# Groups by seven products in a macaron channel mixer: two products accumulate onto banks whose contents were copied, and two splits change place

## The chip, the core and the metric

The kernel runs on one core of one Trainium2 chip. The metric is device time in microseconds of that core, the median of several executions. TensorE (PE) multiplies, VectorE (DVE) and ScalarE (ACT) work elementwise and read what TensorE leaves in PSUM, GpSimd (POOL) and SyncE (SP) mostly issue transfers. PSUM has eight banks of 128 x 512 float32 values here.

## The reference

Two layers over 256 tokens of width 1024. Each layer is a SwiGLU channel mixer at half weight, an attention part, and a second SwiGLU mixer; so there are four passes of the mixer. The change is in the mixer alone:

```
def swiglu(h, w_gate, w_up, w_down):
    return (jax.nn.silu(h @ w_gate) * (h @ w_up)) @ w_down
...
x = x + 0.5 * swiglu(rms_norm(x, ffn1_norm[l]), ffn1_w_gate[l], ffn1_w_up[l], ffn1_w_down[l])
```

`h` is 256 x 1024, the gate and up weights 1024 x 2816, the down weights 2816 x 1024, all float32.

## The kernel before

**Precision.** Every weight and activation is split into a high part (a cast to the fast float format on ScalarE) and a low part (the rest, a subtraction on VectorE). A product is three matmuls for each block of 128: high by high, low by high, high by low. A "split" below is half of a loaded weight block: one cast of 128 x 1024 values on ScalarE and one subtraction of that size on VectorE.

**Groups.** The 2816 hidden columns are taken in five groups of 512 (g = 0 to 4) and a narrow one of 256. Each group makes its hidden block h, and the down projection of a group runs inside the next one. Four PSUM banks hold the output of the down projection for the whole pass; four banks are left for everything else.

**Groups by seven products.** A group's gate and up projections for two blocks of 128 tokens are a two by two block product. In the groups listed in `SEVEN` (2 to 4 in the first pass, 1 to 4 in the other three, 15 in all) it is done with seven products in place of eight, from sums of weights and sums of activations. The weight sums are made by transfers that add on their way (issued by POOL, `gather`) and by additions on VectorE (`plus`); the activation sums by `make_sums`, whose fourth tile is named `v`, so that the seventh product is the only one with `ps<-w,v` in a trace. `prod` makes one product: 12 matmuls into a fresh bank. `by_seven` (line 634) runs for g > 1: first product, copy to m1; seventh product, copy to m7; the transposes of the former h (`turn`, which also splits the down operands: two casts, two low parts); second product, and g0 = second + m1; third product; the first half of the down projection (24 matmuls); fifth and sixth product; u2 = sixth - m1, u3 = m7 + u2; fourth product, g1 = fourth - u3; the last three subtractions and additions with the fifth and third product; the two `up` multiplications that make h; the second half of the down projection. For g = 1 the order differs: first product, half the transposes, second product, the other half, down projection, third product, seventh product with its copy, then fifth, sixth, fourth. g0 passes through SiLU on ScalarE: in the first pass behind the third product, in the other passes behind the first half of the down projection (`run` is true there).

**Order.** In the mixer each engine runs its instructions in the order in which the program text issues them. `weights()` takes the next weight block and calls `ahead(n)`, which issues splits up to number n, the additions that prepare them, and loads into free ones of six raw buffers. Block i has the splits 2i and 2i + 1. A plain `weights()` goes to 2i + look, and the product itself goes one further in its middle (`Split.part`); `held=True` leaves the latter out, and the first argument of `weights` lowers the former. `look` is 8 less one for each group by seven behind the first in passes two to four (8 for g = 1, 5 for g = 4), and 6, then 5, in the first pass. Loads go out on SyncE's queue when a raw buffer is free, and the adding transfers on POOL's.

**Buffers.** m1, m7, g0 and the other 128 x 512 temporaries share five buffers (`tmp`).

Of the kernel before, what the change touches and what calls it, by code (L numbers as in the profile page):

```python
# [12 lines left out]
ALU = mybir.AluOpType  # L13
# [21 lines left out]
def trunk(ctx: ExitStack, tc: tile.TileContext, x, n1, g1, u1, d1, nm, w_in, sink,  # L35
# [21 lines left out]
    pe, act, dve, pool = Kept(nc.tensor), Kept(nc.scalar), Kept(nc.vector), Kept(nc.gpsimd)  # L57
# [9 lines left out]
    def nm_(s):  # L67
        uid[0] += 1
        return f"{s}_{uid[0]}"

    def bank():
        return ps.tile([P, 512], F32, tag="ps", bufs=8, name=nm_("ps"))
# [4 lines left out]
    def blk(dt=F32R):  # L77
        return s4.tile([P, 2, 512], dt, tag="s4", name=nm_("s4"))

    def tmp(tag="tmp", bufs=5, shape=(P, 2, 256), dt=F32):  # L80
        return tp.tile(list(shape), dt, tag=tag, bufs=bufs, name=nm_(tag))
# [143 lines left out]
    look = [IN_MIX]  # L225
    at = dict(use=0, dma=2, prep=2, split=4)
# [22 lines left out]
    def weights(less=0, held=False):  # L249

        i = at["use"]
        at["use"] += 1
        if i > 1:
            ahead(2 * i + look[0] - less)
        w = loaded[i]
        w.held = held
        return w
# [181 lines left out]
    norm = Norm(0)  # L439
# [162 lines left out]
    def ffn(norm, aside=None, before=None, final=False, sevens=SEVEN[1]):  # L602
        def silu(out_, acc, t):
            act.activation(out_, acc, AF.Silu, scale=norm.r[:, t:t + 1])
            return out_

        def gate(gs):
            g = []
            for t in range(2):
                n = gs[t].shape[1]  # L610
                g.append(silu(tmp().rearrange("p a n -> p (a n)")[:, :n], gs[t], t))
            return g

        def up(h, acc, g, t):
            n = acc.shape[1]
            dve.scalar_tensor_tensor(h[:, t, :n], in0=acc, scalar=norm.hr[:, t:t + 1], in1=g, op0=ALU.mult, op1=ALU.mult)

        def hidden(g, us):
            h = blk(F32)
            for t in range(2):  # L620
                up(h, us[t], g[t], t)
            return h

        def prod(xo, w):
            acc = bank()
            for k in range(4):
                hi, lo = w.part(k)
                xh, xl = xo(k)
                pe.matmul(acc, lhsT=xh, rhs=hi, start=k == 0, stop=False)
                pe.matmul(acc, lhsT=xl, rhs=hi, start=False, stop=False)  # L630
                pe.matmul(acc, lhsT=xh, rhs=lo, start=False, stop=k == 3)
            return acc

        def by_seven(h, g):


            flat = lambda: tmp().rearrange("p a n -> p (a n)")

            def put(o, x, y, op):
                dve.tensor_tensor(o, x, y, op=op)  # L640
                return o

            late, run = g == max(sevens), 1 in sevens
            m1, m7 = flat(), flat()
            if g > 1:
                act.copy(m1, prod(norm.quarter(0, 0), weights()))
                act.copy(m7, prod(norm.summed(3), weights(held=True)))
                hT = turn(h, 2)
                p2 = prod(norm.quarter(0, 1), weights())
                g0 = put(flat(), p2, m1, ALU.add)  # L650
                p3 = prod(norm.summed(2), weights())
                if not run:
                    silu(g0, g0, 0)
                down(hT, g - 1, 0, weights())
                if run:
                    silu(g0, g0, 0)
            else:
                p1 = prod(norm.quarter(0, 0), weights(1, True))
                hT = turn(h, (0,))
                w = weights(1, True)  # L660
                act.copy(m1, p1)
                p2 = prod(norm.quarter(0, 1), w)
                hT += turn(h, (1,))
                g0 = put(flat(), p2, m1, ALU.add)
                down(hT, 0, 0, weights())
                silu(g0, g0, 0)
                p3 = prod(norm.summed(2), weights())
                act.copy(m7, prod(norm.summed(3), weights()))
            h = blk(F32)
            p5 = prod(norm.summed(0), weights())  # L670
            p6 = prod(norm.summed(1), weights(look[0] - 5 if late else run, late or run))
            u2 = put(flat(), p6, m1, ALU.subtract)
            u3 = put(m7, m7, u2, ALU.add)
            p4 = prod(norm.quarter(1, 1), weights(look[0] - 4 if late else 3 * run, late or run))
            g1 = put(m1, p4, u3, ALU.subtract)
            w = weights(look[0] - 3 if late else 2 * run)
            silu(g1, g1, 1)
            put(u3, u3, p5, ALU.subtract)
            put(u2, u2, p5, ALU.subtract)
            put(u2, u2, p3, ALU.add)  # L680
            up(h, u2, g0, 0)
            up(h, u3, g1, 1)
            down(hT, g - 1, 1, w)
            return h

        def turn(hs, n):
            out_ = []
            for i in (range(n) if isinstance(n, int) else n):
                sl = halves(bank())
                for c in range(2):  # L690
                    for t in range(2):
                        pe.transpose(sl[:, c, t * P:(t + 1) * P], hs[:, t, (2 * i + c) * P:(2 * i + c + 1) * P], ident)
                hb = blk()
                split(hb, sl)
                out_.append(hb)
            return out_

        accs = [[bank(), bank()] for _ in range(2)]

        def down(hT, g, h, w):  # L700
            tokens(accs[h], [None] * (2 * g) + hT, w, 4 * g, last=(FC - 1, G4 - 1) if final and h else FC - 1)


        gs, us = [bank(), bank()], [bank(), bank()]
        if before is None:
            before = norm.late
        look[0] = IN_FFN
        before(0)
        ws = (weights(), weights(2))
        for k in (0, 2):  # L710
            if k:
                before(1)
                look[0] = IN_FFN + (1 in sevens)
            for sl, w in zip((gs, us), ws):
                tokens(sl, norm.xs, w, 0, (k, k + 1))
                if k and 1 in sevens:
                    norm.copies(2)
        before(2)
        if 1 in sevens:
            sums = norm.make_sums()  # L720
            next(sums)
            norm.halve()
            w = weights()
            next(sums)
            next(sums)
            tokens(gs, norm.xs, w, 4)
            w = weights(0, True)
            g = gate(gs)
            next(sums)
        else:  # L730
            norm.halve()
            tokens(gs, norm.xs, weights(), 4)
            g = gate(gs)
            w = weights()
        tokens(us, norm.xs, w, 4)
        h = hidden(g, us)
        if 1 in sevens:
            next(sums)
        for n in range(1, NGRP):
            if n in sevens:  # L740
                look[0] = IN_FFN + min(sevens) - n if before is not take_x else IN_MIX - (n == NGRP - 1)
                h = by_seven(h, n)
                continue
            sums = norm.make_sums()
            gs = [bank(), bank()]
            tokens(gs, norm.xs, weights(), 0)
            hT = turn(h, 2)
            norm.copies()
            next(sums, None)
            tokens(gs, norm.xs, weights(), 4)  # L750
            g = gate(gs)
            next(sums, None)
            us = [bank(), bank()]
            for k0 in (0, 4):
                tokens(us, norm.xs, weights(), k0)
                next(sums, None)
            h = hidden(g, us)
            for hh in range(2):
                down(hT, n - 1, hh, weights())
                if hh == 0:  # L760
                    next(sums, None)

        gu = [bank(), bank()]
        tokens(gu, norm.xs, weights(), 0)
        hT = turn(h, 2)
        tokens(gu, norm.xs, weights(), 4)
        h = hidden(gate([b[:, 0:256] for b in gu]), [b[:, 256:512] for b in gu])

        def rest():
            hE = turn(h, 1)  # L770
            if aside is not None:
                aside()
            return hE
        return accs, hT, rest
# [294 lines left out]
    for l in range(DEPTH):  # L1069
# [7 lines left out]
        if not final:  # L1077
            norm = Norm((l + 1) * 8)
# [39 lines left out]
    for c in (0, 256):  # L1118
        acc = bank()[:, 0:256]
# [35 lines left out]
```

## Time and profile before

| what | value |
|---|---|
| median of 3 executions | 925.17 us (923.89 to 926.65) |
| profiled execution | 924.94 us |
| its span, first to last instruction | 923.2 us |
| granted TensorE clock | 0.999 of full speed |
| DMA, mean over the span | 218 GB/s |

A row of the timeline gives start, length, engine, line, operation, output and inputs by the program's names (`w` split weights, `raw` loaded weights, `s` activations and hidden blocks, `q` and `v` activation sums, `tmp` temporaries, `ps` PSUM), shapes and a count; in brackets stands the engine's idle time before it and what ended it. Rows of one kind in a run are merged: the length is then that of the run. Since a helper records all instructions, all have line L50; they are told apart by their tiles. Matmuls overlap, so the length of one (0.39 us) is not the step from one to the next.

### The profile page before, as it was taken

How to read it: one execution, taken by the hardware profiler on the slowest of the kernel's cores; microseconds unless marked ns; L12 is line 12 of the kernel's file. 1: busy time of each engine (PE TensorE's matmuls, PEld its weight loads, DVE VectorE, ACT ScalarE, POOL GpSimd, SP SyncE). 2: the span in 40 equal slices, each digit the busy share in tenths (PEclk: the TensorE clock that was granted, in tenths of full speed). 3: DMA queues.
4: the chain of work that ended last, by engine and by line, in shares of the span. 5: the costliest groups of instructions: out<-in, count | busy, mean ns of one | idle time of the engine just before them, and what ended most of it. 6: DMA issues, size and time to landing. Idle time of an engine off the chain costs nothing.

```text
span 923.2 us, 12580 instructions
## 1 busy us (share of the span) xinstructions
PE 908.6 (98%) x4696; PEld 763.7 (83%) x4696; DVE 807.6 (87%) x1123; ACT 590.6 (64%) x917; POOL 67.7 (7%) x83
## 2 busy tenths in 40 slices
PE   8999999999999999999999999999999999999997
PEld 6888888899888888877888888788998888888786
DVE  6769999969875999999879999997698689999995
ACT  7846575557755776575486676565577496676561
POOL 0501000000000100100010010000001010000011
PEclk9999999999999999999999999999999999999999
DMA  9997897837436698897767998787462467998831
GB/s 334 355 235 208 248 273 266 237 101 221 135 123 182 151 287 245 247 269 263 258 168 200 295 264 235 233 288 227 118 232 92 137 155 202 282 279 243 232 135 47
DMA packets 114061, 200.87 MB, mean 218 GB/s; under 512 B 3662, under 2 KB 31376, under 8 KB 114000
## 3 DMA queue, kind: packets, MB, share of 16 engines
q1 hardware_dynamic: 96528, 166.74, 53.6%
q0 software_dynamic: 16096, 31.75, 19.1%
q10 hardware_dynamic: 1376, 1.57, 0.5%
q8 instruction: 37, 0.61, 0.3%
q14 instruction: 24, 0.20, 0.1%
HBM read 199.00 MB, written 1.05 MB: 217 GB/s over the span
## 4 chain that ended last, share of the span: by engine, by line
PE 85%; DVE 11%; issue 2%; DMA 1%; ACT 1%; SPq 0%; POOLq 0%; POOL 0%; DVEq 0%; ACTq 0%
PE ps L50 85%; DVE w L50 7%; DVE raw L50 2%; DVE tmp L50 1%; DVE s L50 1%; DMA raw<-in_ffn_w_gate_dram 1%; ACT w L50 1%; ACT tmp L50 0%; SPq L156 0%; DVE xk L50 0%; POOLq L1150 0%; POOL rf L50 0%; SPq L422 0%; DVEq L50 0%; ACTq L50 0%
## 5 line engine op out<-in xcount | busy, mean ns | idle before, releaser
L50 PE MATMUL ps<-w,s 128*128 128x512 f32 (+1 forms) x2574 | 602.8, 391 | 1.2 <-ACT w L50 0.5
L50 PEld LDWEIGHTS ps<-w,s 128*128 128x128 f32 x2574 | 477.0, 188 | 102.5 <-DVE w L50 4.3
L50 DVE TENSOR_TENSOR w<-raw,w 128x1024 fp32r<-128x1024 f32 (+1 forms) x458 | 482.7, 1102 | 33.7 <-ACT w L50 32.8
L50 ACT CAST w<-raw 128x1024 fp32r<-128x1024 f32 (+1 forms) x458 | 411.0, 953 | 133.0 <-DVE raw L50 94.5
L50 PE MATMUL ps<-w,q 128*128 128x512 f32 x540 | 127.3, 389 | 0.0
L50 PEld LDWEIGHTS ps<-w,q 128*128 128x128 f32 x540 | 101.4, 188 | 21.0
L50 PE MATMUL ps<-s,w 128*128 128x256 f32 x672 | 84.0, 285 | 0.0
L50 PEld LDWEIGHTS ps<-s,w 128*128 128x128 f32 x672 | 81.7, 191 | 1.1
L50 POOL DMA_DIRECT2D raw<-in_ffn_w_up_dram x30 | 38.9, 1295 | 477.0 <-DVE w L50 161.9
L50 DVE TENSOR_TENSOR raw<-raw,raw 128x1024 f32<-128x1024 f32 x60 | 70.7, 1222 | 0.0
L50 ACT ACTIVATE s<-ps,gcol 128x256 fp32r<-128x256 f32 (+1 forms) x80 | 31.7, 479 | 43.8 <-PE ps L50 42.1
L50 PE MATMUL ps<-w,v 128*128 128x512 f32 x180 | 44.1, 391 | 3.0 <-DVE w L50 3.0
L50 PEld LDWEIGHTS ps<-w,v 128*128 128x128 f32 x180 | 33.6, 188 | 11.0 <-DVE w L50 4.2
L50 ACT CAST s<-ps 128x512 fp32r<-128x512 f32 x44 | 24.3, 595 | 26.4 <-PE ps L50 26.4
L50 PE MATMUL ps<-ident,s 128*128 128x128 f32 x304 | 40.5, 273 | 0.0
L50 PEld LDWEIGHTS ps<-ident,s 128*128 128x128 f32 x304 | 35.3, 140 | 5.9 <-issue 0.8
L50 ACT COPY tmp<-ps 128x512 f32<-128x512 f32 x34 | 19.9, 585 | 28.7 <-PE ps L50 21.3
L50 ACT ACTIVATE s<-s,negm 128x256 f32<-128x256 f32 x64 | 31.9, 502 | 6.6 <-DVE negm L50 6.4
L50 DVE TENSOR_TENSOR tmp<-ps,tmp 128x512 f32<-128x512 f32 x49 | 33.7, 687 | 2.5 <-PE ps L50 1.6
L50 DVE TENSOR_TENSOR s<-ps,s 128x512 fp32r<-128x512 f32 x44 | 28.7, 686 | 7.0 <-ACT s L50 7.0
L50 ACT ACTIVATE tmp<-tmp,r 128x512 f32<-128x512 f32 x30 | 21.6, 720 | 16.3 <-DVE tmp L50 16.1
L50 DVE SCALAR_TENSOR_TENSOR s<-ps,gcol,s 128x256 fp32r<-128x256 f32 x48 | 20.3, 479 | 11.3 <-ACT s L50 11.2
(106 smaller groups left out, 409.1 us busy)
## 6 DMA issues: line engine op xcount, KB each, us to landing
raw<-in_ffn_w_down_dram SPq DMA_DIRECT2D x44, 1024.0 KB, 8.5
raw<-in_ffn_w_gate_dram SPq DMA_DIRECT2D x39, 1024.0 KB, 5.6
raw<-in_ffn_w_up_dram SPq DMA_DIRECT2D x39, 1024.0 KB, 5.3
raw<-in_ffn_w_up_dram POOLq DMA_DIRECT2D x30, 1024.0 KB, 11.6
raw<-in_w_in_dram SPq DMA_DIRECT2D x14, 1024.0 KB, 5.3
raw<-in_ffn_w_gate_dram SPq DMA_DIRECT2D x8, 512.0 KB, 4.2
raw<-in_ffn_w_up_dram SPq DMA_DIRECT2D x8, 512.0 KB, 5.3
raw<-in_w_in_dram SPq DMA_DIRECT2D x8, 512.0 KB, 5.4
```

The source lines that it names most:

```text
L50: ins = issue(*a, **k)
```

## The change

`prod` can be given a bank to add to; it then starts no new accumulation. The second product is added onto the first one's bank after m1 was copied from it (g > 1), and the sixth onto the seventh's after m7 was copied (all groups by seven). The combinations of products are rearranged to fit. In g > 1 the seventh product asks for one split less at its start. In g = 3 of passes two to four one split is issued ahead of the two `up`s in place of behind them.

```diff
-        def prod(xo, w):
-            acc = bank()
+        def prod(xo, w, acc=None):
+
+            first = acc is None
+            if first:
+                acc = bank()
             for k in range(4):
                 hi, lo = w.part(k)
                 xh, xl = xo(k)
-                pe.matmul(acc, lhsT=xh, rhs=hi, start=k == 0, stop=False)
+                pe.matmul(acc, lhsT=xh, rhs=hi, start=first and k == 0, stop=False, skip_group_check=not first)
...
             if g > 1:
-                act.copy(m1, prod(norm.quarter(0, 0), weights()))
-                act.copy(m7, prod(norm.summed(3), weights(held=True)))
+                g0 = prod(norm.quarter(0, 0), weights())
+                act.copy(m1, g0)
+                p7 = prod(norm.summed(3), weights(1, True))
+                act.copy(m7, p7)
                 hT = turn(h, 2)
-                p2 = prod(norm.quarter(0, 1), weights())
-                g0 = put(flat(), p2, m1, ALU.add)
+                prod(norm.quarter(0, 1), weights(), g0)
                 p3 = prod(norm.summed(2), weights())
                 if not run:
-                    silu(g0, g0, 0)
+                    g0 = silu(flat(), g0, 0)
                 down(hT, g - 1, 0, weights())
                 if run:
-                    silu(g0, g0, 0)
+                    g0 = silu(flat(), g0, 0)
...
-                act.copy(m7, prod(norm.summed(3), weights()))
+                p7 = prod(norm.summed(3), weights())
+                act.copy(m7, p7)
             h = blk(F32)
             p5 = prod(norm.summed(0), weights())
-            p6 = prod(norm.summed(1), weights(look[0] - 5 if late else run, late or run))
-            u2 = put(flat(), p6, m1, ALU.subtract)
-            u3 = put(m7, m7, u2, ALU.add)
+            prod(norm.summed(1), weights(look[0] - 5 if late else run, late or run), p7)
+            u1 = put(m1, p7, m1, ALU.subtract)
             p4 = prod(norm.quarter(1, 1), weights(look[0] - 4 if late else 3 * run, late or run))
-            g1 = put(m1, p4, u3, ALU.subtract)
+            g1 = put(flat(), p4, u1, ALU.subtract)
             w = weights(look[0] - 3 if late else 2 * run)
             silu(g1, g1, 1)
-            put(u3, u3, p5, ALU.subtract)
-            put(u2, u2, p5, ALU.subtract)
-            put(u2, u2, p3, ALU.add)
-            up(h, u2, g0, 0)
-            up(h, u3, g1, 1)
+            put(u1, u1, p5, ALU.subtract)
+            u0 = put(m7, u1, m7, ALU.subtract)
+            put(u0, u0, p3, ALU.add)
+            if run and g == max(sevens) - 1:
+                ahead(2 * at["use"] - 2 + look[0] - 1)
+            up(h, u0, g0, 0)
+            up(h, u1, g1, 1)
             down(hT, g - 1, 1, w)
```

More of the change, by code (lines that the diff above doesn't have):

```diff
@@ L628, in prod @@
                 xh, xl = xo(k)
-                pe.matmul(acc, lhsT=xh, rhs=hi, start=k == 0, stop=False)
-                pe.matmul(acc, lhsT=xl, rhs=hi, start=False, stop=False)
-                pe.matmul(acc, lhsT=xh, rhs=lo, start=False, stop=k == 3)
+                pe.matmul(acc, lhsT=xh, rhs=hi, start=first and k == 0, stop=False, skip_group_check=not first)
+                pe.matmul(acc, lhsT=xl, rhs=hi, start=False, stop=False, skip_group_check=not first)
+                pe.matmul(acc, lhsT=xh, rhs=lo, start=False, stop=k == 3, skip_group_check=not first)
             return acc
```

## The prediction

> **What bounds the kernel now.** I read the page first: TensorE is busy nearly all the span and the chain that ended last lies on it.
>
> ```profile
> span 923.2 us, 12580 instructions
> PE 908.6 (98%) x4696; PEld 763.7 (83%) x4696; DVE 807.6 (87%) x1123; ACT 590.6 (64%) x917; POOL 67.7 (7%) x83
> PE 85%; DVE 11%; issue 2%; DMA 1%; ACT 1%; SPq 0%; POOLq 0%; POOL 0%; DVEq 0%; ACTq 0%
> ```
>
> So a VectorE instruction taken away is worth nothing unless TensorE waited for it. The view of waits says how often TensorE did: its weight loads waited for the low parts of the split weights (DVE w).
>
> ```profile
> PEld ps L50 <- DVE w L50: 8.6, 13, 1.8
> ```
>
> Thirteen waits in 923 us. To place and price them I took the timeline of TensorE. The eight transposes (or four and four in the first group by seven of a pass) stand once in each group; from one row of eight to the next lie 7 products of 12 matmuls, 48 matmuls of the down projection and 8 transposes. The same count lies between the last group by seven and the narrow group behind it.
>
> ```profile
> 345.28 1.03 PE L50 MATMUL ps<-ident,s 128*128 128x128 f32 x8
> ...
> 376.13 1.03 PE L50 MATMUL ps<-ident,s 128*128 128x128 f32 x8
> ...
> 408.86 1.03 PE L50 MATMUL ps<-ident,s 128*128 128x128 f32 x8
> ...
> 440.29 1.04 PE L50 MATMUL ps<-ident,s 128*128 128x128 f32 x8
> ...
> 131.85 1.04 PE L50 MATMUL ps<-ident,s 128*128 128x128 f32 x8
> ...
> 163.41 1.03 PE L50 MATMUL ps<-ident,s 128*128 128x128 f32 x8
> ...
> 554.22 1.03 PE L50 MATMUL ps<-ident,s 128*128 128x128 f32 x8
> ...
> 586.21 1.04 PE L50 MATMUL ps<-ident,s 128*128 128x128 f32 x8
> ...
> 617.69 1.04 PE L50 MATMUL ps<-ident,s 128*128 128x128 f32 x8
> ...
> 829.97 1.03 PE L50 MATMUL ps<-ident,s 128*128 128x128 f32 x8
> ...
> 861.81 1.04 PE L50 MATMUL ps<-ident,s 128*128 128x128 f32 x8
> ...
> 893.28 1.04 PE L50 MATMUL ps<-ident,s 128*128 128x128 f32 x8
> ```
>
> 345.28 to 376.13 is 30.85 us: a group in which TensorE hardly waits. The others differ from it by what it waited: second pass 32.73 and 31.43, so 1.88 + 0.58; first pass 31.56, so 0.71; third 31.99 and 31.48, so 1.14 + 0.63; fourth 31.84 and 31.47, so 0.99 + 0.62. Together 6.55 us, all at the end of a pass. That is the most that relief of VectorE can bring in these groups. Why at the end: VectorE falls behind a little in each group and lives on the splits made ahead, which shrink by one a group (`look`).
>
> **The change, part by part.** The costs of one instruction:
>
> ```profile
> L50 DVE TENSOR_TENSOR w<-raw,w 128x1024 fp32r<-128x1024 f32 x354 | 415.2, 1221 | 27.2 <-ACT w L50 26.4
> L50 DVE TENSOR_TENSOR tmp<-ps,tmp 128x512 f32<-128x512 f32 x49 | 33.7, 687 | 2.5 <-PE ps L50 1.6
> L50 DVE TENSOR_TENSOR tmp<-tmp,tmp 128x512 f32<-128x512 f32 x15 | 10.4, 693 | 0.5
> L50 ACT ACTIVATE tmp<-tmp,r 128x512 f32<-128x512 f32 x30 | 21.6, 720 | 16.3 <-DVE tmp L50 16.1
> L50 ACT ACTIVATE tmp<-ps,r 128x512 f32<-128x512 f32 x10 | 6.4, 698 | 0.0
> ```
>
> *Second product onto the first one's bank* (12 groups, those with g > 1). It takes away one VectorE add of 0.687 us a group. The SiLU of g0 now reads PSUM (0.698 for 0.720 us, ScalarE, nothing). The second product's first matmul must wait for the copy of m1; that copy is long done:
>
> ```profile
> 373.60 0.59 ACT L50 COPY tmp<-ps 128x512 f32<-128x512 f32 x1 [0.65 <-PE ps L50]
> ```
>
> It ends at 374.19 and the second product starts behind the transposes of 376.13, some 0.8 later: 2.7 us of seventh product and transposes cover it. Without that cover it would cost 0.6 us a group.
>
> *Sixth product onto the seventh one's bank* (15 groups). It takes away the add u3 (0.693 us, the fifteen of the row above), and one subtraction changes its source from PSUM to SBUF, which the two rows price alike. With the 12 adds before that is 27 instructions, 27 x 0.69 = 18.6 us less VectorE work. For g > 1 the seventh product is copied a whole half group ahead. For g = 1 (passes two to four) the order is third, seventh, fifth, sixth, and only the fifth product lies between:
>
> ```profile
> 325.50 4.14 ACT L50 CAST w<-raw 128x1024 fp32r<-128x1024 f32 x4 [1.80 <-DVE raw L50]
> 326.24 5.60 PE L50 MATMUL ps<-w,q 128*128 128x512 f32 x24
> 329.54 0.58 ACT L50 COPY tmp<-ps 128x512 f32<-128x512 f32 x1
> ...
> 507.64 0.57 ACT L50 COPY tmp<-ps 128x512 f32<-128x512 f32 x1
> 509.77 11.04 PE L50 MATMUL ps<-w,s 128*128 128x512 f32 x48
> ```
>
> The 24 matmuls from 326.24 are the fifth and sixth product; one takes (5.60 - 0.39)/23 = 0.227 us, 0.39 being the shown length of a single one, so the sixth starts at 326.24 + 12 x 0.227 = 328.96. The copy ends at 330.12, because ScalarE takes four casts first, which waited for VectorE's sums of raw weights. Today that lateness frees a bank nobody needs; after the change TensorE stands 1.16 us. The third pass has the same: sixth product from 509.77 - 2.72 = 507.05, copy until 508.21, again 1.16. Nothing edited lies ahead of that copy in such a group. A restart costs more (four matmuls behind a stall, below, take 1.19 - 0.39 = 0.80 for three steps instead of 0.68), so 1.16 + 0.04 + 0.12 = 1.3 us, three times: 3.9 us lost. The 0.04 is an estimate of the step from copy to matmul, from the stall row below (VectorE's first split is over at 407.8, the matmul starts at 407.83).
>
> *A matmul that waits for something long done.* No row prices it alone. Bounds: nothing, as no matmul is saved, and 0.12 x 27 = 3.2 us if each were a restart. I take nothing: the row of 24 above crosses from one product, with its own waits, to the next without a break.
>
> *One split less ahead of the seventh product* (12 groups). The split moves behind the two low parts of the down operands, with its cast on ScalarE; these come 1.22 us sooner. It is needed: the first and seventh product now hold their banks on, so the third product must take one of the two banks of the transposes, and that is free only when its low part is made.
>
> ```profile
> 374.85 5.76 DVE L50 TENSOR_TENSOR w<-raw,w 128x1024 fp32r<-128x1024 f32 x5
> 379.73 2.88 PE L50 MATMUL ps<-w,q 128*128 128x512 f32 x12
> 380.53 1.29 DVE L50 TENSOR_TENSOR s<-ps,s 128x512 fp32r<-128x512 f32 x2
> ...
> 393.33 11.36 PE L50 MATMUL ps<-w,s 128*128 128x512 f32 x48
> 393.69 0.72 ACT L50 ACTIVATE tmp<-tmp,r 128x512 f32<-128x512 f32 x1
> ```
>
> In this group, the worst, the first low part ends at about 381.2, 1.5 after the third product's start. Four splits instead of five bring it to 380.0, and the stall of 1.3 us in g = 1 moves TensorE to 381.0: in time. The fourth product likewise needs the bank that g0 holds until its SiLU, at 394.41, 1.08 after that product's start at 393.33; the add taken away (0.6) and TensorE's 1.3 put it ahead by 0.8. If either cover goes, TensorE waits here in the same places of nine groups.
>
> The moved split also frees a weight buffer later, and SP and POOL are behind it:
>
> ```profile
> 349.04 0.37 SPq L153 DMA_DIRECT2D raw<-in_ffn_w_up_dram  x1
> 354.71 1.28 POOL L50 DMA_DIRECT2D raw<-in_ffn_w_up_dram  x1 [19.60 <-DMA raw<-in_ffn_w_up_dram]
> 366.54 2.00 ACT L50 CAST w<-raw 128x1024 fp32r<-128x1024 f32 x2 [0.99 <-DMA raw<-in_ffn_w_up_dram]
> 368.08 3.49 DVE L50 TENSOR_TENSOR w<-raw,w 128x1024 fp32r<-128x1024 f32 x3
> ```
>
> The load of 349.04 goes out at the end of the fifth split; two low parts later (1.2), so do the adding transfer of POOL and the cast of 366.54: 367.7, its split at 368.8, 0.7 later than now. TensorE's 1.3 covers it; without that, this eats the one group's gain.
>
> *A split ahead of the ups* in g = 3 of passes two to four. It is the one that TensorE stood for:
>
> ```profile
> 404.53 1.98 PE L50 MATMUL ps<-w,v 128*128 128x512 f32 x8
> 405.23 1.41 DVE L50 SCALAR_TENSOR_TENSOR s<-tmp,hr,tmp 128x512 f32<-128x512 f32 x2
> 406.56 5.76 DVE L50 TENSOR_TENSOR w<-raw,w 128x1024 fp32r<-128x1024 f32 x5
> 407.83 1.19 PE L50 MATMUL ps<-w,v 128*128 128x512 f32 x4 [1.33 <-DVE w L50]
> ```
>
> Eight matmuls end their turn at 404.53 + 8 x 0.227 = 406.35; the ninth starts 1.48 later, when the first of five splits is over. Ahead of the ups that split starts at 405.23 and ends at 406.45 even if VectorE were no earlier. The ups end 1.2 later, at 407.8; they are wanted by the transposes, 408.86 now, 408.86 - 1.6 + 1.3 = 408.6 then: covered. The new SiLU and g1 buffers leave four of five temporaries in use a group, as now: nothing.
>
> **Sum.** VectorE gains 0.6 to 1.3 us a group, the waits at the ends of the passes go: -6.55. Sixth product in g = 1: +3.9. The rest nothing. The profiled execution took 924.94 (span 923.2 and 1.7 around it); 924.94 - 6.55 + 3.9 = 922.3. The median of the runs is 925.17, 0.2 above the profiled one; I keep 922.3.
>
> **Rivals.** *Banks, slower.* The third or the fourth product waits in the nine groups g = 2 to 4 of passes two to four. It decides when a low part, or g0's SiLU, comes later than the product that wants the bank; or when the planner hands the fourth product the bank of the seventh. For it: 1.5 and 1.08 us of lateness in the rows above. Against it: 1.2 + 1.3 us of shift. Its full price is (1.08 + 0.12) x 9 = 10.8; I take half, as the other groups are less late: 922.3 + 5.4 = 927.7. The Trainium skill, Perfetto Trace Analysis, section Matmuls, speaks for this: independent matmul groups should rotate through different PSUM banks, so that evacuation of one overlaps the next. Here two chains give up their rotation. By that rule each of 27 accumulations pays about a copy (0.59), 16 us; the trace agrees for g = 1 alone (1.16 late) and not for g > 1 (2.7 early).
>
> *Transfers.* The load chain above takes back what VectorE gains, and half of the waits stay: 922.3 + 3.3 = 925.6. For it: 0.99 us of wait for a transfer already now. Against it: only one cast a group hangs on it.
>
> *The copy is not late.* ScalarE reaches it 1.2 us sooner, the 3.9 falls away: 918.4. Against it: the four casts and their wait are untouched.
>
> **How the numbers follow.** Forecast 0.58, with its own range 920.8 to 924.0; banks 0.20; transfers 0.10; copy not late 0.12. 0.3% of 925.17 is 2.8, about what a measurement of this kernel tells from no change, so faster means below 922.4: of the forecast 0.33, and the copy's 0.12. Within: 0.25 of the forecast and 0.07 of the transfers. Slower: banks 0.20 and 0.03 of the transfers. The range runs from 918.4 up to 928: the lower rival, and the bank rival at its half price.
>
> **What would show it.** Right: no wait for DVE w before the seventh product's ninth matmul in g = 4; rows of transposes 30.9 apart to the end of each pass; a TensorE wait for ACT tmp of 1.2 to 1.3 us ahead of the sixth product in g = 1, three times; 27 fewer VectorE instructions. Wrong: TensorE waiting for DVE s or for the SiLU ahead of the third or fourth product, group after group; or waits for DVE w as before, with ScalarE waiting longer for the up weights.

## The result and the profile after

The median went from 925.26 us (923.89 to 926.65, 13 runs) to 922.48 us (922.08 to 924.38, 13 runs): a ratio of 0.9974, 95% interval 0.9965 to 0.9982, or 2.8 us less where 2.9 were forecast. The profiled execution took 922.74 us against 924.94, 2.2 less; the sum of the prediction, which was made up from the profiled execution, had 2.65 (-6.55 + 3.9). So the two terms together were 0.4 us off, and that the medians come out at 2.8 for 2.9 is partly luck. The prediction took 0.3% as the least that counts as faster and gave 0.45 to faster and 0.32 to within; the ratio, 0.26% below 1, lies within, though its interval excludes 1.

The page of the changed kernel: span, busy times, the chain that ended last, and the group of additions whose first operand is in PSUM.

```profile
span 921.0 us, 12546 instructions
PE 906.9 (98%) x4696; PEld 763.7 (83%) x4696; DVE 793.5 (86%) x1096; ACT 589.5 (64%) x917; POOL 66.1 (7%) x83
PE 92%; DVE 4%; ACT 2%; issue 1%; DMA 1%; SPq 0%; POOLq 0%; POOL 0%; ACTq 0%
L50 DVE TENSOR_TENSOR tmp<-ps,tmp 128x512 f32<-128x512 f32 x37 | 25.4, 686 | 8.6 <-PE ps L50 8.4
```

VectorE has the 27 instructions less (1096 for 1123), and by its groups 18.6 us less of them: 8.3 in the one shown (25.4 for 33.7) and 10.3 in those with PSUM as second operand (15 fewer, 0.684 each). Its busy time, which counts overlapping lengths once, fell by 14.1. The chain shows what became of it: VectorE's share is 4% where it was 11%, TensorE's 92% where it was 85%. The last row shows it from VectorE's side: ahead of these instructions it now stands idle for 8.6 us, nearly all of it until TensorE is done, where it stood 2.5 us before. It has caught up with TensorE.

The view of waits, rows of TensorE (PE) and of its weight loads (PEld): total us, times, longest.

```profile
PEld ps L50 <- ACT tmp L50: 6.0, 6, 1.5
PE ps L50 <- ACT tmp L50: 3.6, 4, 1.0
...
PEld ps L50 <- DVE w L50: 1.2, 4, 0.4
...
PEld ps L50 <- DVE s L50: 0.4, 2, 0.2
```

The waits for low parts of weights fell from 8.6 us in 13 times to 1.2 in 4; waits for ScalarE's temporaries, 0.8 us in 2 times before, are now the largest row. Two engines' rows of one wait overlap (a weight load and its matmul both stand), so places and prices come from the timeline. First the transposes, whose distances are the lengths of the groups by seven:

```profile
131.95 1.05 PE L50 MATMUL ps<-ident,s 128*128 128x128 f32 x8
...
162.99 1.04 PE L50 MATMUL ps<-ident,s 128*128 128x128 f32 x8
...
346.19 1.03 PE L50 MATMUL ps<-ident,s 128*128 128x128 f32 x8
...
377.03 1.03 PE L50 MATMUL ps<-ident,s 128*128 128x128 f32 x8
...
407.85 1.04 PE L50 MATMUL ps<-ident,s 128*128 128x128 f32 x8
...
438.69 1.03 PE L50 MATMUL ps<-ident,s 128*128 128x128 f32 x8
...
553.88 1.04 PE L50 MATMUL ps<-ident,s 128*128 128x128 f32 x8
...
584.73 1.03 PE L50 MATMUL ps<-ident,s 128*128 128x128 f32 x8
...
615.75 1.04 PE L50 MATMUL ps<-ident,s 128*128 128x128 f32 x8
...
829.43 1.03 PE L50 MATMUL ps<-ident,s 128*128 128x128 f32 x8
...
860.24 1.04 PE L50 MATMUL ps<-ident,s 128*128 128x128 f32 x8
...
891.09 1.03 PE L50 MATMUL ps<-ident,s 128*128 128x128 f32 x8
```

In order: 31.04 in the first pass; 30.84, 30.82, 30.84 in the second; 30.85, 31.02 in the third; 30.81, 30.85 in the fourth. The groups of 31.56, 32.73, 31.43, 31.99, 31.48, 31.84 and 31.47 us are gone. Taken group by group, that is 0.52 + 1.91 + 0.59 + 1.14 + 0.46 + 1.03 + 0.62 = 6.27 us won.

Then the timeline of the second pass's g = 1, TensorE and ScalarE around the sixth product:

```profile
325.06 4.13 ACT L50 CAST w<-raw 128x1024 fp32r<-128x1024 f32 x4 [1.81 <-DVE raw L50]
325.81 2.88 PE L50 MATMUL ps<-w,q 128*128 128x512 f32 x12
329.10 0.58 ACT L50 COPY tmp<-ps 128x512 f32<-128x512 f32 x1
329.73 3.02 PE L50 MATMUL ps<-w,q 128*128 128x512 f32 x12 [1.04 <-ACT tmp L50]
```

The unbroken 24 matmuls of the fifth and sixth product have become 12 and 12. The sixth starts 329.73 - 325.81 = 3.92 us behind the fifth, where 12 steps of 0.227 are 2.72: a stand of 1.20, and it ends with the copy (329.68). From the fifth product to the transposes of the next group it was 345.28 - 326.24 = 19.04 us and is 346.19 - 325.81 = 20.38: the group is 1.34 longer, the restart included. So 3 x 1.34 = 4.0 us were given back of the 6.27, and 2.2 are left, which is the difference of the spans.

### The profile page after: what moved, and what is told of

The parts are those of the page before. It is cut to its first block, busy times and chain, and to the rows that moved or that the text cites. A ratio compares the mean times of both kernels' runs of the same rounds, so it can differ in the third digit from the quotient of the medians.

```text
span 921.0 us, 12546 instructions
## 1 busy us (share of the span) xinstructions
PE 906.9 (98%) x4696; PEld 763.7 (83%) x4696; DVE 793.5 (86%) x1096; ACT 589.5 (64%) x917; POOL 66.1 (7%) x83
## 3 DMA queue, kind: packets, MB, share of 16 engines
q0 software_dynamic: 16096, 31.75, 19.2%
## 4 chain that ended last, share of the span: by engine, by line
PE 92%; DVE 4%; ACT 2%; issue 1%; DMA 1%; SPq 0%; POOLq 0%; POOL 0%; ACTq 0%
PE ps L50 92%; DVE w L50 2%; DVE raw L50 1%; ACT w L50 1%; DMA raw<-in_ffn_w_gate_dram 1%; ACT tmp L50 0%; DVE s L50 0%; DVE tmp L50 0%; ACT s L50 0%; SPq L156 0%; DVE xk L50 0%; ACT L50 0%; POOLq L1158 0%; POOL rf L50 0%; SPq L422 0%
## 5 line engine op out<-in xcount | busy, mean ns | idle before, releaser
L50 DVE TENSOR_TENSOR tmp<-ps,tmp 128x512 f32<-128x512 f32 x37 | 25.4, 686 | 8.6 <-PE ps L50 8.4
L50 DVE TENSOR_TENSOR xk<-xk,ps 128x512 f32<-128x512 f32 (+1 forms) x25 | 14.1, 597 | 15.1 <-PE ps L50 15.1
```

The lines of the kernel that those rows point to most:

```text
L50: ins = issue(*a, **k)
```

## The experiments

Two pairs of theories were to be told apart. On the copy of m7: *ledger* says that the stand at the sixth product and the relief at the ends of the passes are terms on their own, so without the stand all of its 4 us come back; *cover* says that this stand is also what keeps the low parts and g0's SiLU ahead of TensorE, so that part of it returns elsewhere. On the relief: *work* says that it comes from the VectorE instructions taken away; *order* says that it comes from the splits that change place. The kernel before ran beside them on the same chips with medians of 924.6 to 924.8 us; ratios are to it, and one thousandth is 0.92 us.

**The copy made twice** (e9). In g = 1 the copy of m7 is issued a second time with the same result, so that the stand is longer by a known amount.

```diff
                 act.copy(m7, p7)
+                act.copy(m7, p7)
```

> The changed kernel with the copy of m7 made twice for g = 1 (the same values again), so that the sixth product waits for the second of them. If the copy stands on the path of TensorE as the ledger has it, each of the three waits grows by one copy on ScalarE, 0.5 to 0.6 us: 922.5 + 1.6 = 924.1, and the trace shows waits for ACT tmp of 1.7 us where it had 1.2. If ScalarE's lateness were only a label in the trace and something else released the product, the waits and the time stay: 922.5.

924.06 us, ratio 0.9992 (0.9983 to 1.0000), 0.0018 or 1.7 us above the change. Its timeline at the same place:

```profile
328.61 1.19 ACT L50 COPY tmp<-ps 128x512 f32<-128x512 f32 x2
329.85 3.02 PE L50 MATMUL ps<-w,q 128*128 128x512 f32 x12 [1.66 <-ACT tmp L50]
```

TensorE stands 1.66 us in place of 1.04, by 0.62 more; three times that is 1.9. What the copy is late is paid one to one.

**The copy ahead of the casts** (e1). The seventh product of g = 1 issues fewer splits at its start, so that fewer casts stand ahead of the copy in ScalarE's queue.

```diff
-                p7 = prod(norm.summed(3), weights())
+                p7 = prod(norm.summed(3), weights(1, True))
                 act.copy(m7, p7)
```

> The changed kernel with one edit: for g = 1 the seventh product asks for no split at its start and none in its middle, so that ScalarE has the copy of m7 in front of two casts instead of behind them. Ledger theory (the change took 6 us of waits at the ends of the passes away and put in three waits of 1.3 us for that copy): the copy ends about 2 us sooner, before the sixth product wants the bank, the three waits go, 922.5 - 4.0 = 918.5. Cover theory (the rival: the three waits were also the cover for the banks of the third and fourth product): TensorE then waits for DVE s or for the SiLU in g = 2 to 4 of passes two to four, and 1 to 4 us come back, 919.5 to 922.5.

919.94 us, 0.9952 (0.9939 to 0.9965). Against the change that is 0.0022, 2.0 us of the 4.0. The timeline, g = 1 of the second pass and then g = 3 of the third:

```profile
325.67 5.60 PE L50 MATMUL ps<-w,q 128*128 128x512 f32 x24
327.08 0.58 ACT L50 COPY tmp<-ps 128x512 f32<-128x512 f32 x1
...
567.79 0.68 ACT L50 ACTIVATE tmp<-ps,r 128x512 f32<-128x512 f32 x1
568.52 1.66 PE L50 MATMUL ps<-w,s 128*128 128x512 f32 x6
```

The copy is over at 327.66, the sixth product starts at 325.67 + 2.72 = 328.39, and the 24 matmuls are one row again: the stand is gone. But now the fourth product starts at 568.52, when g0's SiLU has just ended (568.47). That is the wait of the bank rival, 0.2 us here and 0.2 once more in the last pass, where splits are late behind it too. The transposes give the price:

```profile
856.33 1.04 PE L50 MATMUL ps<-ident,s 128*128 128x128 f32 x8
...
887.94 1.03 PE L50 MATMUL ps<-ident,s 128*128 128x128 f32 x8
```

This group, the last of the fourth pass, has 31.61 us; one of the third pass has 31.19 (551.07 to 582.26) and the one ahead in the fourth 30.93 (825.40 to 856.33); the change had 30.85, 30.85 and 30.81. The three groups with g = 1 are 4.0 us shorter in all, 1.2 come back in these three, and the residue of 0.4 that the change still had is gone: 3.2, the difference of the two spans (917.8 and 921.0). The ratio says 2.0, but its interval is 2.4 wide. So cover's mechanism is there, and its price in this execution is 1.2 us, not 2.

**An own bank for the sixth product in g = 1** (e2). The stand is taken away by undoing one accumulation, with one VectorE addition more in three groups.

```diff
-            prod(norm.summed(1), weights(look[0] - 5 if late else run, late or run), p7)
-            u1 = put(m1, p7, m1, ALU.subtract)
+            p6 = prod(norm.summed(1), weights(look[0] - 5 if late else run, late or run), p7 if g > 1 else None)
+            u1 = put(m1, p6, m1, ALU.subtract)
+            if g == 1:
+                put(u1, u1, m7, ALU.add)
```

> The changed kernel, but for g = 1 the sixth product has a bank of its own again, and VectorE one more addition (m7) in those three groups. Ledger theory: the three waits go as in the run before, 3 x 0.69 us of VectorE work come back where it has slack, 918.5. If the order of ScalarE's queue mattered beyond the copy, this run and the one before would differ by more than 1 us. Cover theory: as in the run before, 919.5 to 922.5.

920.11 us, 0.9941 (0.9928 to 0.9954): 3.1 us better than the change by the ratios. Its view of waits:

```profile
PEld ps L50 <- DVE s L50: 3.0, 6, 0.7
...
PE ps L50 <- DMA xk<-in_x_dram: 2.3, 2, 2.0
```

The weight loads wait for low parts of the down operands (DVE s) six times, 3.0 us, where the change had 0.4: the other half of the bank rival, the third product or the transposes. Only two of the six (0.3 and 0.7, at 585.13 and 589.13) lie behind a stand that this edit took away; the other four lie in the first pass, which has no g = 1 by seven and is not edited here, so they are the difference between two executions. This execution took 922.92, above its own median: its first transposes stand 0.85 us later than the change's (the opening, with 2.3 us for the first transfer of x), and its first pass is 1.5 longer. With the stand gone, both banks named in the prediction come late in some groups of the later passes.

**The split ahead of the ups, alone** (e5). The kernel before, with that one part of the change.

```diff
             put(u2, u2, p3, ALU.add)
+            if run and g == max(sevens) - 1:
+                ahead(2 * at["use"] - 2 + look[0] - 1)
             up(h, u2, g0, 0)
```

> The kernel before with one part of the change alone: the split ahead of the two ups in g = 3 of passes two to four. Work theory (the waits at the ends of the passes come from VectorE having more to do in a group than TensorE): the wait of 0.9 to 1.5 us in the seventh product of g = 4 goes, and as VectorE has the same work, the waits ahead of the fourth product of g = 4 grow by about as much; nothing is gained, 925, within 0.7. Order theory (the rival: the split only stood in the wrong place): 1.5 + 1.1 + 0.9 = 3.5 us go and stay away, 921.5.

924.50 us, 0.9996 (0.9987 to 1.0004): nothing that can be told from none. The timeline of the end of the second pass:

```profile
404.82 2.90 PE L50 MATMUL ps<-w,v 128*128 128x512 f32 x12
405.22 1.22 DVE L50 TENSOR_TENSOR w<-raw,w 128x1024 fp32r<-128x1024 f32 x1
...
425.51 1.23 DVE L50 TENSOR_TENSOR w<-raw,w 128x1024 fp32r<-128x1024 f32 x1
...
426.80 1.43 PE L50 MATMUL ps<-w,s 128*128 128x512 f32 x5 [0.53 <-DVE w L50]
```

The seventh product now runs its 12 matmuls in one row. But twenty microseconds later the fourth product stands longer for its splits. The two groups that had 32.73 and 31.43 us have 30.83 and 32.71 (transposes at 376.73, 407.56 and 440.27). Over the three passes their waits go from 5.8 to 5.0 us, so the order is worth 0.9 us at most in these two executions. VectorE, once behind, stays behind here, and its order mostly chooses which product pays: work holds, and order falls but for a small part.

**The change without that split** (e3).

```diff
             put(u0, u0, p3, ALU.add)
-            if run and g == max(sevens) - 1:
-                ahead(2 * at["use"] - 2 + look[0] - 1)
             up(h, u0, g0, 0)
```

> The changed kernel without the split issued ahead of the two ups in g = 3 of passes two to four. Ledger theory: with the additions gone VectorE has the split ready at about 405.7 even behind the ups, and the ninth matmul of the seventh product wants it at 406.9, so nothing changes: 922.5, within 0.5. Order theory (the rival: the moved splits, not the missing additions, took the waits away): the wait of about 1.2 us before that matmul returns in each of three passes, 922.5 + 3.5 = 926.

922.82 us, 0.9982 (0.9973 to 0.9990), not to be told from the change's 0.9974. Its waits of TensorE for ScalarE's temporaries are the three copies alone, and there is no row of TensorE waiting for low parts of weights at all:

```profile
PE ps L50 <- ACT tmp L50: 3.1, 3, 1.0
```

**The seventh product as before** (e4). The change with the split put back ahead of the down operands' low parts.

```diff
-                p7 = prod(norm.summed(3), weights(1, True))
+                p7 = prod(norm.summed(3), weights(held=True))
```

> The changed kernel with the moved split back ahead of the seventh product in g > 1. The low parts of the down operands then come 1.2 us later. Ledger theory: the third product waits for its bank where the first low part ended less than 1.2 us ahead of it in the changed kernel: g = 3 of pass one by 0.7, g = 4 of passes one and three by 0.4, each with 0.1 for the restart, 922.5 + 1.8 = 924.3. Order theory: waits for split weights or for low parts in most groups, more than 4 us, over 926.5. If the move did nothing: 922.5.

924.04 us, 0.9990 (0.9982 to 0.9999): 0.0016 or 1.5 us lost. Its view of waits, and the timeline in g = 4 of the third pass:

```profile
PEld ps L50 <- DVE s L50: 2.4, 3, 1.1
```

```profile
588.52 1.28 DVE L50 TENSOR_TENSOR s<-ps,s 128x512 fp32r<-128x512 f32 x2
589.26 0.98 PE L50 MATMUL ps<-w,q 128*128 128x512 f32 x3 [0.67 <-DVE s L50]
```

The third product starts inside the pair of low parts, when the first of them (588.52 + 0.64) has freed its bank. This is the rival's wait in the very place the prediction named, and what the moved split prevents; it came in three groups, not in nine, and two of the three are those that the expectation names (the third is g = 4 of the fourth pass, in place of the first). No wait for low parts of weights stands in this view either: they are gone without the moved split, and the split earns its 1.5 us at the banks.

**Second product's accumulation alone** (e6): the change, with the sixth product in its own bank in all groups.

```diff
-            prod(norm.summed(1), weights(look[0] - 5 if late else run, late or run), p7)
-            u1 = put(m1, p7, m1, ALU.subtract)
+            p6 = prod(norm.summed(1), weights(look[0] - 5 if late else run, late or run))
+            u1 = put(m1, p6, m1, ALU.subtract)
+            put(u1, u1, m7, ALU.add)
```

> The changed kernel, but the sixth product has a bank of its own in all groups, and VectorE the 15 additions of m7 again; both moved splits stay. Ledger theory: the three copy waits go (-4.0); VectorE is still relieved of 12 additions, 1.8 us by the end of a pass, so of the 6.0 us at the ends 0.7 returns in pass two: 919 to 919.5. Cover theory: with the copy waits gone the fourth product waits for g0's SiLU by 0.2 to 1 us in some of the nine groups, 920 to 922.

920.92 us, 0.9958 (0.9946 to 0.9969). Its waits:

```profile
PEld ps L50 <- ACT tmp L50: 2.6, 7, 0.6
PEld ps L50 <- DVE w L50: 2.5, 8, 0.4
```

Twelve additions less, with both moved splits, bring the low parts of weights from 8.6 us of waiting (longest 1.8) to 2.5 (longest 0.4). With no stand to cover it, the fourth product waits for SiLU again, which is the rest of the first row.

**Sixth product's accumulation alone** (e7): the change, with the second product in its own bank.

```diff
-                prod(norm.quarter(0, 1), weights(), g0)
+                p2 = prod(norm.quarter(0, 1), weights())
+                g0 = put(flat(), p2, m1, ALU.add)
...
-                    g0 = silu(flat(), g0, 0)
+                    silu(g0, g0, 0)
```

> The changed kernel, but the second product has its own bank again and VectorE the 12 additions that make g0; both moved splits and the sixth product on the seventh's bank stay. Ledger theory: three copy waits of 1.3 us as in the changed kernel, which also give VectorE that time, and 15 additions less; the ends of the passes stay nearly free of waits: 922.5 to 923.5, nothing like twice as good or bad as the changed kernel. If the first kind of accumulation carried the gain: about 925.

924.04 us, 0.9996 (0.9988 to 1.0005): no gain, about 1 us worse than expected. It has the three stands in full, and a residue of the old waits:

```profile
PE ps L50 <- ACT tmp L50: 3.1, 3, 1.0
PEld ps L50 <- DVE w L50: 2.9, 8, 1.0
```

So fifteen instructions less also relieve VectorE of most of its lateness, though not by a figure that can be put beside e6's: here the three stands give VectorE time as well. The copy in g = 1 takes the gain back. Of the two accumulations tried alone, only the second product's earns anything. Whether the whole change is even slower than e6 is not settled: the intervals overlap (0.9965 to 0.9982, 0.9946 to 0.9969).

**SiLU earlier** (e8, e10, e11). If cover is right, e1 and e2 gain more when g0's SiLU no longer comes behind the down projection. All three put it right behind the second product: e8 on e1, e10 on e1 without the split ahead of the ups, e11 on e2.

```diff
                 prod(norm.quarter(0, 1), weights(), g0)
+                g0 = silu(flat(), g0, 0)
                 p3 = prod(norm.summed(2), weights())
-                if not run:
-                    g0 = silu(flat(), g0, 0)
                 down(hT, g - 1, 0, weights())
-                if run:
-                    g0 = silu(flat(), g0, 0)
```

> The first experiment (copy of m7 ahead of the casts for g = 1) with one more edit: for g > 1 g0's SiLU is issued right behind the second product, in place of behind the first half of the down projection, so that its bank is free some 10 us before the fourth product wants one. Cover theory: the waits for the SiLU ahead of the fourth product that the first experiment's trace shows in passes three and four (0.2 each with the restarts 0.3 to 0.7) go: 0.5 to 1.0 us less than it, 919.0 to 919.5. Ledger theory without cover: the same as the first experiment, 919.9.

> The eighth experiment (copy of m7 ahead of the casts for g = 1, SiLU of g0 right behind the second product) without the split ahead of the two ups. Ledger theory: as in the third experiment nothing hangs on that split, 919.5 within 0.7. Order theory: with the copy waits gone the ninth matmul of the seventh product in g = 4 wants the split at about 405.5 and has it at 404.9 in pass two but only just in pass four, so waits of up to 0.3 us come back there: 920.

> The second experiment (a bank of its own for the sixth product of g = 1, with the addition of m7 back there) with the SiLU of g0 right behind the second product for g > 1. Ledger theory: both ways round the copy wait are worth the same, and the early SiLU takes the 0.2 us waits ahead of the fourth product: 919.0 to 920.0, equal to the eighth experiment within 0.7.

919.45 us, 0.9946 (0.9935 to 0.9958); 920.05 us, 0.9943 (0.9930 to 0.9956); 919.74 us, 0.9938 (0.9924 to 0.9952). Waits of weight loads in e8:

```profile
PEld ps L50 <- DVE w L50: 1.5, 3, 1.0
...
PEld ps L50 <- DVE s L50: 1.1, 3, 0.5
```

The waits for SiLU are gone (the weight loads' waits for ScalarE's temporaries are 0.8 us again, as in the kernel before), but the time is e1's within the intervals, and e11's is e2's. Waits of 0.2 us are too little to be seen in medians, and other waits came: in e8 the last group of the fourth pass has 32.31 us (856.72 to 889.03), mostly for splits; in e10 the seventh product of the third pass stands for a split again (582.36), the wait that the order theory named, though in one group only, of another pass, which has 31.54. The five kernels without the stand (e1, e2, e8, e10, e11) can't be told from each other; all are some 0.5 to 0.6% faster than the kernel before, and e11 has the lowest ratio.

## Why the prediction was right, step by step

**Waits at the ends of the passes: -6.55 forecast, -6.27 measured.** The residue is 0.2 us in the first pass (31.04) and 0.17 in the third (31.02). What removed them is, in the main, VectorE's work: e5 moves a split and leaves VectorE's work as it was, and gains 0.9 us at most; e3 and e4 each take one of the moved splits back, and the waits for low parts of weights stay away; e6 and e7 keep both moved splits and each give a part of the work back, and a part of the waits returns (2.5 and 2.9 us of weight loads, for 8.6 before). No run takes both moved splits back at once.

**Copy in g = 1: 1.3 each forecast, 1.34 measured.** The copy was seen to be late where nobody waited for it, and its lateness became TensorE's stand. e9 confirms the price by lengthening it, e1 and e2 by its removal (30.4 us from the second transposes of that group to the next, as before; 31.75 in the change). The rival that the copy would not be late fell: the four casts and their wait for VectorE's sums stand ahead of it at 325.06 as they stood at 325.50.

**By pass** the sums held but for the first. The same transposes stand 0.42 us sooner at the end of the first pass (163.41 and 162.99), 1.60 at the end of the second (440.29 and 438.69), 1.94 of the third (617.69 and 615.75) and 2.19 of the fourth (893.28 and 891.09). So the first pass gave 0.42 where 0.71 was forecast (0.2 is the residue, 0.1 the opening), the second 1.18 where 1.88 + 0.58 - 1.3 = 1.16 were forecast, the third 0.34 for 0.47, the fourth 0.25 for 0.31.

**Matmuls that wait for something long done: nothing.** The groups of the changed kernel have 30.81 to 30.85 us with two accumulations in each, against 30.85 before with none; the upper bound of 0.12 for each would have made 31.09. The trace shows no price where the copy lies 2.7 us ahead, and 1.2 us where it is late. The Trainium skill (Perfetto Trace Analysis, section Matmuls) says that independent matmul groups should rotate through different PSUM banks; the prediction read from it a price of about a copy for each accumulation, and this trace agrees for g = 1 alone.

**The moved split and the two banks.** Third and fourth product of the second pass's g = 3, with what frees their banks:

```profile
378.39 1.28 DVE L50 TENSOR_TENSOR s<-ps,s 128x512 fp32r<-128x512 f32 x2
380.64 2.88 PE L50 MATMUL ps<-w,q 128*128 128x512 f32 x12
...
392.37 0.67 ACT L50 ACTIVATE tmp<-ps,r 128x512 f32<-128x512 f32 x1
394.24 3.11 PE L50 MATMUL ps<-w,s 128*128 128x512 f32 x13
```

The first low part is done at 379.03, 1.6 ahead of the third product, where 1.0 was forecast; SiLU at 393.04, 1.2 ahead of the fourth, where 0.8 was. Without the move (e4) the third product waits, without the stand (e1, e2) both do here and there. So the bank rival was a real mechanism, held off by the covers that the prediction named. The prediction said that with either cover gone TensorE waits in nine groups; with one gone it waited in three (e1, e2, e4) to five (e6), and in e4 that is 2.4 us of weight loads' waits. No run takes both covers away.

**Transfers.** The load chain of the moved split, SyncE, POOL, ScalarE, VectorE:

```profile
350.18 0.37 SPq L153 DMA_DIRECT2D raw<-in_ffn_w_up_dram  x1
...
355.63 1.28 POOL L50 DMA_DIRECT2D raw<-in_ffn_w_up_dram  x1 [20.95 <-DMA raw<-in_ffn_w_up_dram]
...
366.36 2.00 ACT L50 CAST w<-raw 128x1024 fp32r<-128x1024 f32 x2 [1.49 <-PE ps L50]
366.95 3.49 DVE L50 TENSOR_TENSOR w<-raw,w 128x1024 fp32r<-128x1024 f32 x3
```

The load goes out 1.14 us later, as worked out, and the adding transfer 0.92 later. There the step failed: the cast was to come at 367.7, 1.2 later, and it came at 366.36, 0.18 sooner than before. The prediction also misread the split. It took the first of the row at 368.08 for the split of this cast; but by the order of casts and splits it is the second, at about 369.2 before, and at about 368.1 now, as the first starts at 366.95, before the cast is over. The lateness was not passed on (last section). It cost nothing either way, so the sum was not touched.

**Split ahead of the ups.** Priced at nothing for the ups, it was called the one that TensorE stood for. In the changed kernel TensorE doesn't stand there with it or without it (e3):

```profile
403.22 1.22 DVE L50 TENSOR_TENSOR w<-raw,w 128x1024 fp32r<-128x1024 f32 x1
...
405.12 2.89 PE L50 MATMUL ps<-w,v 128*128 128x512 f32 x12
```

VectorE comes to this split at 403.22, 2.0 us sooner than it came to the ups before; the seventh product itself only starts at 405.12.

**What the prediction left out.** It added the two terms as if they were independent. For the change as made that is right. For the next step it isn't: taking the stand away brought 2.0 to 3.3 us of 4.0 by the ratios, in five kernels. The traces show where the rest is. In all five the groups with g = 1 are together 4.0 us shorter than the change's. The other groups of passes two to four, each against the 30.83 us of one without waits, are longer by 1.2 us together in e1, 2.1 in e2, 1.7 in e8 and 0.7 in e10 and e11. With the stand in place it is 0.2 in the change and nothing in e3 and e9. So the stand, which also gives VectorE 1.3 us in each of these passes, covered 0.5 to 1.9 us of other waits, one execution of each kernel being traced.

## What to carry to other kernels

An engine off the critical path that falls behind by a little in each round can show up as waits at the end of a series only, as here; instructions taken from it are worth those waits and no more, and reordering its work mostly moved the wait to the next consumer. Accumulating onto a bank that was copied was free in this kernel where the copy was over by the time the product came round, and cost the copy's lateness and a restart where it wasn't, so look up each place where the copy stands in its engine's queue, not the typical one. A stall that is taken away uncovers the next ones: read in the trace what ended just in time before counting on all of it.

## What the runs showed that I had not expected

The adding transfer of POOL went out 0.92 us later and was over no later. The view of transfers of the same load, before and after (kilobytes, us from issue to landing):

```profile
raw<-in_ffn_w_up_dram POOLq DMA_DIRECT2D x1, 1024.0 KB, 11.7
```

```profile
raw<-in_ffn_w_up_dram POOLq DMA_DIRECT2D x1, 1024.0 KB, 10.6
```

Before, it was issued 0.07 us ahead of the next gate load (354.71 and 354.78); after, 0.91 behind it (355.63 and 354.72). Whether this order made the difference, no run tried.

The opening of the program differs from one execution to the next by as much as some of the edits are worth: the first row of transposes starts at 36.66 us before, 36.73 after, and between 36.19 (e7) and 37.58 (e2). TensorE's stand at about 30 us in the first pass isn't there in the profile of before. In the changed kernel's it was idle there for 0.45 us until a temporary of ScalarE's came, in e10 for 1.3; the wait for the first transfer of x was 0.8 us before, 0.7 after and 2.3 in e2. It is part of the spread of the runs (918.5 to 922.9 in e2), and one reason why versions that differ by under 2 us were left untold apart.
